# A hybrid convolution and pooling trunk on one core: turning the second group's frames on VectorE by way of memory, with two weight pieces finished by accumulating transfers

## Chip, cores and metric

One core of a Trainium2 chip runs the whole program. The metric is the device time of one execution, in microseconds; the time before is the median of three runs. A profiled execution has a span (first to last instruction) and a time of its own, which is a little longer.

## What is computed

One layer over 2,048 frames of a new stream and 32 frames of a running one, 1,024 channels each:

```python
hn = rmsnorm(h, g_mix)
hA, bA, cA, zA, vB, zB = split(hn @ w_in)              # six projections of 512 columns
u = cA * hA;  c = causal width-3 convolution of u       # yA = bA * c * silu(zA)
pooled = trailing mean of vB over 2, 4, 8 or 16 frames - vB
yB = (pooled @ pool_w[group]) * pool_scale * silu(zB)   # four groups of 128 channels
h = h + concat(yA, yB) @ w_out
h = h + (p @ w_ple) * sigmoid(rmsnorm(h, g_ple) @ w_ple_gate)
y = rmsnorm(h, g_final)
```

Besides y, the last rows of u and vB of both streams are returned.

## The kernel before

**Numbers.** Each float32 operand of a product is split into an upper part (the value cast to fp32r, by ScalarE) and a lower part (value minus upper part, by VectorE); `split` at L76 issues both. A product is three matmuls: upper by upper, upper by lower, lower by upper.

**Frames.** The 2,080 frames are five blocks of 416 columns, in three groups: blocks 0 and 1, blocks 2 and 3, block 4 (with the running stream). For the input projections a group's normalized frames must stand transposed in SBUF, channels on partitions. For a two-block group they are kept as seven operands with four quarters combined (halves of the channels by the two blocks): 11, 21, 22 and four differences T1 to T4, each split.

**Units and pairs.** A group has four units j, one for each 128 columns of every projection. A unit's six projections are made in three pairs, zb/v, c/h and za/b (`pair`, L859). A pair takes seven *half products* (`half_product`, L560) of 12 matmuls of 416 columns instead of eight, into three PSUM banks X, Y and Z. The weights' seven pieces (11, 12, S2, S1, S3, S4, 22) are made from two raw tiles of 512 KB by `pair_weights` (L521): differences on VectorE, then a split into a piece of a ring of seven buffers (`wr`); raw tiles come from a ring of four (`raws`). ScalarE's `carry` (L871) and VectorE's `out` (L874) read the banks between the products; TensorE goes on accumulating into a bank only after they have read it. Unit 0 of the first group (`plain`) multiplies in the ordinary way.

**The second group's frames.** While units 1 to 3 of the first group run, the generator `next_columns` (L1049) prepares the seven operands of the second group, 128 columns at a time, first the short last column (32 frames of each block), then columns 0, 1 and 2. `at_pace(..., 39, 62)` at L1154 advances it between half products. A column goes: load the frames of both blocks, sum of squares on ScalarE, root on GpSimd, scaling in place on VectorE (`normal`, L407), 16 transposes on TensorE into PSUM (`turn` and `four`; 8 for the short column), then the differences and seven splits, each written to memory by GpSimd (`to_memory`, L482). At the start of the second group, `load_group` loads the operands back. Frames, turned tiles and staged splits share a ring of five 4 KB slots (`xin`).

**The third group's frames** go another way already (`last_block`): `scaled_to_memory` (L1091) scales in four strided parts and writes to memory, `from_memory` (L1102) reads the rows back so that each 32-row block lies in the partitions where it belongs, and `turned_in_place` (L1110) turns all 32x32 blocks with one VectorE instruction.

**Pooling weights.** `pool_w` is loaded at once, 256 KB, and split in `vectors` (L660); `mix` (L719) multiplies a unit's pooled values with it, three matmuls a block.

**Order.** The program is written in one order, and a scheduler with its own costs puts the instructions of each engine into the order in which they run; `keep_in_program_order` holds single instructions to the written order. On the chip every engine, and each DMA queue (SP's and GpSimd's), issues strictly in that order.

Of the kernel before, what the change touches and what calls it, by code (L numbers as in the profile page):

```python
# [9 lines left out]
F32 = mybir.dt.float32  # L10
# [19 lines left out]
EARLY = 3  # L30
LATE = 2
LATER = 4


@with_exitstack
def trunk(ctx, tc, x_p, x_s, c_conv, c_pool, p_p, p_s, g_mix, w_in, conv_w, conv_b, pool_w,
# [29 lines left out]

    def rstd_of(ssq, n, name, r=None):

        ms = sm.tile([P, 1], F32, tag="ms", name=f"ms_{name}")
        nc.gpsimd.tensor_scalar(ms[:n], ssq[:n], scalar1=1.0 / D, scalar2=EPS,  # L70
                                op0=ALU.mult, op1=ALU.add)
# [259 lines left out]
    with ExitStack() as s1:  # L331
# [21 lines left out]
        def ftile(name):  # L353
            return wk.tile([P, KH, P], F32, tag="f", bufs=4, name=name)
# [73 lines left out]
        def four(xs, tag):  # L428

            for half in range(2):  # L430
                if len(xs) == 2:
                    yield [turn(x, half, f"pt_{tag}_{i}_{half}", later=True) for i, x in enumerate(xs)]
                else:
                    t = turn(xs[0], half, f"pt_{tag}_{half}", later=True)
                    yield [t[:, :, :DEC], t[:, :, DEC:2 * DEC]]

        def frame_sums(xs, tag, dst):
# [20 lines left out]
            p21, p22 = next(steps)  # L458
            nc.scalar.copy(f21, p21)
            sub(f1, p22, f1)  # L460
            sub(f12, p22, f12)
            dst("21", p21, n)
            yield
            dst("22", p22, n)
            yield
            dst("T2", f1, n)
            sub(f21, f21, f1)
            yield
            dst("T3", f12, n)
            yield  # L470
            dst("T4", f21, n)
            yield


# [7 lines left out]

        def to_memory(mem, name, src, at, n, t=None, later=False):
            t = t or staged(name)[:, :, :, :n]
            ins = put(t, src)
# [44 lines left out]
        def pair_weights(gi, ka, kb, j, name, ring, s_ring):  # L530

            s_t = (wk.tile([P, KH, P], F32, tag="s", bufs=1, name=f"s_{name}") if s_ring is None else
                   s_ring(f"s_{name}"))
            ra = raw_weight(ka, j, f"{name}a", ring)
            a11, a12 = ra[:, :KH], ra[:, KH:]
            sub = lambda o, x, y: nc.vector.tensor_tensor(o, x, y, op=ALU.subtract)
            rb = raw_weight(kb, j, f"{name}b", ring)  # L540
            a21, a22 = rb[:, :KH], rb[:, KH:]
            ins = nc.vector.tensor_tensor(s_t, a21, a22, op=ALU.add)
            if (gi, ka, j) == (1, "za", 0):
                tc.keep_in_program_order(ins)
            sub(a21, a11, a21)
            s3 = a21
            src = {"11": a11, "12": a12, "S2": a11, "S1": s_t, "S3": s3, "S4": a12, "22": a22}

            def make(q):
                if q == "S2":  # L550
                    sub(a11, s_t, a11)
                if q == "S4":
                    sub(a12, a12, a11)
                t = wtile(f"w_{name}_{q}")
                put(t, src[q])
                return t

            return make
# [84 lines left out]


        vec = const.tile([P, 112], F32, name="vec")
        pw = one.tile([P, 2, 4, P], F32R, name="pw")
# [9 lines left out]
        def vectors():  # L656
            pv = tbank("pv")
            tc.keep_in_program_order(nc.tensor.transpose(pv[:, :112], rows, ident[:112, :112]))
            nc.vector.tensor_copy(vec, pv[:, :112])
            split(pw[:, 0], pw[:, 1], pw_raw)  # L660

        cw = lambda r, j: vec[:, r * 4 + j:r * 4 + j + 1]
        cb = lambda j: vec[:, 12 + j:13 + j]
# [4 lines left out]
        pw_raw = raws.tile([P, 4, P], F32, tag="t", name="raw_pw")  # L668
        nc.sync.dma_start(pw_raw, pool_w[0].rearrange("g c d -> c g d"))

        def etile(name, n=NB):
            return wk.tile([P, 2 * NB + 16], F32, tag="e", bufs=2, name=name)[:, :n]
# [1 line left out]
        class Unit:  # L674


            def __init__(self, gi, tbs, j):
                self.gi, self.tbs, self.j, self.tag = gi, tbs, j, f"{gi}_{j}"
                self.L = min(SEQ - tbs[0] * NB, len(tbs) * NB)
                self.last = tbs[-1] == 4  # L680
                self.pooled = None
                t = lambda name, n: big.tile([P, n], F32, tag=name, name=f"{name}_{self.tag}")
# [32 lines left out]
            def store(self, chunk, b, t):  # L715
                r = self.tbs[b] * NB
                nc.sync.dma_start(y_d[chunk, :, r:r + NB], self.cols(t, b))

            def mix(self, b):  # L719

                pp, j = self.cols(self.pooled.rearrange("p h n -> p (h n)"), b), self.j
                pq = self.pooled[:, 1, b * NB:b * NB + NB]
                pm = tbank(f"pm_{self.tag}_{b}")
                nc.tensor.matmul(pm[:, :NB], pw[:, 0, j], pp, start=True, stop=False)
                nc.tensor.matmul(pm[:, :NB], pw[:, 0, j], pq, start=False, stop=False)
                nc.tensor.matmul(pm[:, :NB], pw[:, 1, j], pp, start=False, stop=True)
# [132 lines left out]
            def pair(self, ka, kb, B, D, done, ring, s_ring=None):  # L859
# [34 lines left out]
                yield  # L894
                half_product(X, make("22"), B["T4"], False)
                done[1, 0](X[:, :NB])
                yield

            def seven(self, B, aside, both=False):
# [54 lines left out]
                while i < 3:  # L954
# [4 lines left out]
                    for n in range(8):  # L959
                        for st in steps:  # L960
                            next(st)
                            aside()
                        if n == (0 if both else LATER):
                            while i and late:
                                tc.keep_in_program_order(split(*late.pop()))
                        if both and i == 2 and n == 3:
                            for b in range(2):
                                self.mix(b)
# [78 lines left out]
        def next_columns(*cs):  # L1047

            load_ahead(1, cs[0])  # L1049
            for c, after in zip(cs, cs[1:] + (None,)):  # L1050

                places = iter(t[:, :, :, i * DEC:(i + 1) * DEC] for t in map(staged, ("short_0", "short_1")) for i in range(4))
                dst = lambda q, src, n: to_memory(p_d[q], f"{q}_1_{c}", src, c * P, n, next(places) if n == DEC else None, True)
                for i, _ in enumerate(frame_sums(ahead.pop((1, c)), f"g1_{c}", dst)):
                    if after is not None and i in (6, 7):
                        load_half_ahead(after)
                    yield

# [69 lines left out]
        for gi, tbs in enumerate(GROUPS):  # L1128
# [17 lines left out]
            for j in range(4):  # L1146
                unit = gi * 4 + j
                u = Unit(gi, tbs, j)
                if unit == 0:
# [452 lines left out]
```

## Time and profile before

| | us |
|---|---|
| median of 3 runs (lowest to highest) | 926.43 (925.31 to 927.96) |
| the profiled execution's own time | 927.1 |
| its span | 925.3 |
| unit 1 of the first group begins | 78.5 |
| second group begins | 232.7 |

The profile's rows name the line, the engine (PE = TensorE, PEld its weight loads, DVE = VectorE, ACT = ScalarE, POOL = GpSimd, SP = SyncE's DMA queue), the operation and the tiles. A timeline row starts with the start and the length in us; the length of several merged instructions runs from the first start to the last end. In rows of waits the numbers are the total in us, how often, and the longest. A row of a stretch gives each engine's busy us with the number of instructions, the granted TensorE clock, the DMA engines' share and GB/s.

### The profile page before, as it was taken

Reading aid. Unit: us, or ns where it says so; the run is one execution under the profiler, and the core shown is the slowest. Engines: PE = TensorE matmul, PEld = TensorE weight load, DVE = VectorE, ACT = ScalarE, POOL = GpSimd, SP = SyncE. Lnnn points to the kernel's source line nnn. Section 1 sums busy time; section 2 is a strip of 40 time slices with the busy share of each in tenths; the row PEclk is TensorE's granted clock in tenths of the full one; section 3 lists DMA queues with packets and bytes.
Section 4 is the critical chain, followed back from the end, with each engine's and each line's share of the span. In section 5 each row is a group of like instructions: output and inputs, shape, how many; then the busy total and the mean of one; then the engine's idle time right before and its main releaser. Section 6 shows DMA issues by size and latency. Waiting matters only on the chain. (4 is left out here: it accounts for less than half of the span.)

```text
span 925.3 us, 12917 instructions
## 1 busy us (share of the span) xinstructions
PE 907.0 (98%) x4479; PEld 819.9 (89%) x4479; DVE 722.8 (78%) x1225; ACT 476.2 (51%) x880; POOL 152.8 (17%) x276
## 2 busy tenths in 40 slices
PE   7999999999999999999999999999999999999996
PEld 5999999999999999999999987888877868888884
DVE  6896898999488989785777679665554799888965
ACT  6744556554345455443545456334334776565554
POOL 3110222312001111000000010111111002333324
PEclk8999999999999999999999999999999999999998
DMA  8345555859955646357755359756775886799882
GB/s 245 87 152 153 167 160 178 265 154 317 411 165 174 191 155 189 100 180 277 201 169 173 125 192 289 263 186 177 251 220 167 292 259 160 190 232 232 227 240 91
DMA packets 140654, 186.37 MB, mean 201 GB/s; under 512 B 12044, under 2 KB 111244, under 8 KB 139309
## 3 DMA queue, kind: packets, MB, share of 16 engines
q1 hardware_dynamic: 120093, 126.07, 44.4%
q0 software_dynamic: 17760, 53.97, 19.8%
q10 hardware_dynamic: 2736, 5.51, 1.8%
q8 instruction: 35, 0.57, 0.3%
q14 instruction: 30, 0.25, 0.1%
HBM read 128.93 MB, written 56.56 MB: 200 GB/s over the span
## 5 line engine op out<-in xcount | busy, mean ns | idle before, releaser
L78 ACT CAST y_S<-y_fS 128x512 fp32r<-128x512 f32 x32 | 19.5, 621 | 41.9 <-PE x_o L168 18.9
L103 PE MATMUL e<-wq,pps 128*128 128x512 f32 (+1 forms) x156 | 38.9, 399 | 0.2 <-ACT pps L78 0.2
L168 PE MATMUL x_o<-wo_b,y_S 128*128 128x512 f32 x128 | 35.8, 391 | 0.0
L168 PE MATMUL x_g<-wg_b,g_S 128*128 128x512 f32 x128 | 35.7, 389 | 0.0
L564 PE MATMUL x_zbv<-B,w_zbv_S 128*128 128x416 f32 x168 | 34.2, 352 | 0.0
L564 PE MATMUL x_zab<-B,w_zab_S 128*128 128x416 f32 x168 | 34.1, 351 | 0.0
L564 PE MATMUL x_ch<-B,w_ch_S 128*128 128x416 f32 x168 | 34.1, 351 | 0.0
L564 PE MATMUL z_zab<-B,w_zab_S 128*128 128x416 f32 x168 | 34.0, 351 | 0.0
L564 PE MATMUL z_zbv<-B,w_zbv_S 128*128 128x416 f32 x168 | 34.0, 351 | 0.0
L564 PE MATMUL z_ch<-B,w_ch_S 128*128 128x416 f32 x168 | 34.0, 350 | 0.0
L103 PEld LDWEIGHTS e<-wq,pps 128*128 128x128 f32 (+1 forms) x156 | 27.4, 182 | 6.9 <-ACT pps L78 0.5
L1391 POOL DMA_DIRECT2D e<-h_d x28 | 24.8, 907 | 52.3 <-DVE e L1388 45.3
L70 POOL TENSOR_SCALAR ms_x<-ssq_x 128x1 f32<-128x1 f32 (+2 forms) x18 | 10.7, 592 | 127.5 <-ACT junk L89 127.2
L564 PEld LDWEIGHTS z_zbv<-B,w_zbv_S 128*128 128x128 f32 x168 | 31.4, 188 | 0.3
L564 PEld LDWEIGHTS z_zab<-B,w_zab_S 128*128 128x128 f32 x168 | 31.4, 188 | 0.3
L564 PEld LDWEIGHTS z_ch<-B,w_ch_S 128*128 128x128 f32 x168 | 31.4, 188 | 0.3
L564 PEld LDWEIGHTS x_zab<-B,w_zab_S 128*128 128x128 f32 x168 | 31.3, 188 | 0.4
L564 PEld LDWEIGHTS x_ch<-B,w_ch_S 128*128 128x128 f32 x168 | 31.3, 188 | 0.3
L564 PEld LDWEIGHTS x_zbv<-B,w_zbv_S 128*128 128x128 f32 x168 | 31.3, 188 | 0.4
L78 ACT CAST y<-y 128x512 fp32r<-128x512 f32 x24 | 14.8, 619 | 29.6 <-PE x_o L168 14.0
L168 PEld LDWEIGHTS x_o<-wo_b,y_S 128*128 128x128 f32 x128 | 23.9, 188 | 5.2 <-ACT c_o L1194 0.3
L168 PEld LDWEIGHTS x_g<-wg_b,g_S 128*128 128x128 f32 x128 | 24.0, 188 | 5.0
(582 smaller groups left out, 2649.9 us busy)
## 6 DMA issues: line engine op xcount, KB each, us to landing
y<-y_d SPq DMA_DIRECT2D x16, 512.0 KB, 6.3
x<-in_x_prompt_dram SPq DMA_DIRECT2D x16, 512.0 KB, 5.5
h_d<-x SPq DMA_DIRECT2D x16, 512.0 KB, 2.6
hn<-h_d SPq DMA_DIRECT2D x61, 128.0 KB, 6.7
xt<-in_x_prompt_dram SPq DMA_DIRECT2D x15, 512.0 KB, 7.4
e<-e_d SPq DMA_DIRECT2D x15, 512.0 KB, 5.9
e<-h_d POOLq DMA_DIRECT2D x28, 256.0 KB, 6.8
out_dram<-e POOLq DMA_DIRECT2D x14, 512.0 KB, 3.9
```

What stands on the lines that cost most here:

```text
L70: nc.gpsimd.tensor_scalar(ms[:n], ssq[:n], scalar1=1.0 / D, scalar2=EPS, op0=ALU.mult, op1=ALU.add)
L78: ins = nc.scalar.copy(hi, src)
L103: nc.tensor.matmul(ps[:n], pps[:, a, k, :n], wp[k][b][:, cs], start=k + q == 0, stop=k == 1 and q == 2)
L168: nc.tensor.matmul(ps[:n], lhs[:, k, a, :n], w[b][:, k], start=start and k + q == 0, stop=k == KH - 1 and q == 2, skip_group_check=True)
L564: nc.tensor.matmul(ps[:, :NB], lhs[:, k, x], b[:, k, y], start=start and k + q == 0, stop=stop and k == KH - 1 and q == 2, skip_group_chec ...
L1391: nc.gpsimd.dma_start(ee, h_d[r:r + P, at[1] * NH:at[1] * NH + NH], accum_op=ALU.add)
```

## The change

It has four parts.

1. **Frames of the second group.** `frame_sums` no longer uses TensorE: each frame tile is scaled by `scaled_to_memory` (four strided parts, a write of the tile), read back by `from_memory` (four loads of 128 KB) and turned by one VectorE instruction. `four` is gone, and with it 56 transposes, and ScalarE's two copies out of PSUM a column; the differences are formed from SBUF, in four tiles. The memory tile `xs_d` grows from 416 to 1,664 rows. The pace of the generator goes from 39 to 43 of 62.
2. **Slots.** `xin` has six buffers instead of five, and the tag `ms` four of its own.
3. **Pooling weights.** Each of the twelve units loads its own 64 KB and splits them: in units of pairs beside the late splits of the pooled values, else in `mix`.
4. **Two weight pieces.** In the first group's pairs, pieces S3 and 22 get their lower part otherwise: ScalarE casts the upper part, then writes its negative into the lower part, and a transfer issued by GpSimd adds the raw values to it in SBUF. They are made earlier in the written order: S3 after the product of S2, 22 after that of S1.

```diff
+BY_SUM = "S3", "22"
...
-        xin = frames_in.enter_context(tc.tile_pool(name="xin", bufs=5, side="right"))
+        xin = frames_in.enter_context(tc.tile_pool(name="xin", bufs=6, side="right"))
...
+        whole = lambda t: t.rearrange("p k (g t) -> p k g t", t=32)
+        def frame_sums(xs, tag, rows, dst):
             xs = [x_stat(x, True) for x in xs]
             yield
-            for x in xs:
-                normal(x)
+            for x, r in zip(xs, rows):
+                scaled_to_memory(x, r)
                 yield
+            ts = [from_memory(r, x[1]) for x, r in zip(xs, rows)]
+            yield
             n = P if len(xs) == 2 else DEC
-            f12, f1, f21 = (ftile(f"{c}_{tag}")[:, :, :n] for c in ("f12", "f1", "f21"))
+            f1, f2, f3, f4 = (whole(ftile(f"f{c}_{tag}")[:, :, :n]) for c in range(1, 5))
             sub = lambda o, x, y: nc.vector.tensor_tensor(o, x, y, op=ALU.subtract)
-            steps = four(xs, tag)
-            p11, p12 = next(steps)
-            nc.scalar.copy(f12, p12)
-            sub(f1, f12, p11)
+            u = turned_in_place(ts[0])
+            p11, p21 = u[:, :KH, :n // DEC], u[:, KH:, :n // DEC]
             dst("11", p11, n)
             yield
+            if len(xs) == 2:
+                u = turned_in_place(ts[1])
+            else:
+                u = u[:, :, 1:]
+            p12, p22 = u[:, :KH], u[:, KH:]
+            sub(f1, p12, p11)
             dst("T1", f1, n)
...
+                if gi == 0 and q in BY_SUM:
+                    hi, lo = t[:, :, 0], t[:, :, 1]
+                    nc.scalar.copy(hi, src[q])
+                    nc.scalar.mul(lo, hi.bitcast(F32), -1.0)
+                    nc.gpsimd.dma_start(lo.bitcast(F32), src[q], accum_op=ALU.add)
+                else:
+                    put(t, src[q])
...
+                self.pw = one.tile([P, 2, P], F32R, tag="pw", name=f"pw_{self.tag}")
+                self.pw_raw = one.tile([P, P], F32, tag="pr", name=f"pr_{self.tag}")
+                nc.sync.dma_start(self.pw_raw, pool_w[0, j])
...
                 half_product(X, make("S2"), B["T2"], False)
                 carry(X, (0, 1))
+                w = {"S3": make("S3")} if self.gi == 0 else {}
                 yield
                 half_product(Z, make("S1"), B["T1"], True)
                 carry(Z, (1, 1))
+                if self.gi == 0:
+                    w["22"] = make("22")
                 yield
-                half_product(X, make("S3"), B["T3"], False)
+                half_product(X, w.get("S3") or make("S3"), B["T3"], False)
...
-        xs_d = tc.dram_tile([NB, D], F32, name="xs_d")
+        xs_d = tc.dram_tile([4 * NB, D], F32, name="xs_d")
...
-                    aside = at_pace(next_columns(3, 0, 1, 2), 39, 62)
+                    aside = at_pace(next_columns(3, 0, 1, 2), 43, 62)
```

More of the change, by code (lines that the diff above doesn't have):

```diff
@@ L67, in rstd_of @@
     def rstd_of(ssq, n, name, r=None):
-        ms = sm.tile([P, 1], F32, tag="ms", name=f"ms_{name}")
+        ms = sm.tile([P, 1], F32, tag="ms", bufs=4, name=f"ms_{name}")
         nc.gpsimd.tensor_scalar(ms[:n], ssq[:n], scalar1=1.0 / D, scalar2=EPS,
@@ L426, in columns_in @@
             return [x_load(f"{a}_3", [x_rows(a, 3), x_rows(b, 3)])]
[L428 to L437, printed above, removed]
+        whole = lambda t: t.rearrange("p k (g t) -> p k g t", t=32)
+        def frame_sums(xs, tag, rows, dst):
             xs = [x_stat(x, True) for x in xs]
             yield
-            for x in xs:
-                normal(x)
+            for x, r in zip(xs, rows):
+                scaled_to_memory(x, r)
                 yield
+            ts = [from_memory(r, x[1]) for x, r in zip(xs, rows)]
+            yield
             n = P if len(xs) == 2 else DEC
-            f12, f1, f21 = (ftile(f"{c}_{tag}")[:, :, :n] for c in ("f12", "f1", "f21"))
+            f1, f2, f3, f4 = (whole(ftile(f"f{c}_{tag}")[:, :, :n]) for c in range(1, 5))
             sub = lambda o, x, y: nc.vector.tensor_tensor(o, x, y, op=ALU.subtract)
-            steps = four(xs, tag)
-            p11, p12 = next(steps)
-            nc.scalar.copy(f12, p12)
-            sub(f1, f12, p11)
+            u = turned_in_place(ts[0])
+            p11, p21 = u[:, :KH, :n // DEC], u[:, KH:, :n // DEC]
             dst("11", p11, n)
             yield
+            if len(xs) == 2:
[4 more added lines that the diff above has]
+            sub(f1, p12, p11)
             dst("T1", f1, n)
             yield
[L458 to L461, printed above, removed]
+            sub(f2, p22, f1)
+            sub(f3, p22, p12)
             dst("21", p21, n)
             yield
+            sub(f4, p21, f2)
             dst("22", p22, n)
             yield
-            dst("T2", f1, n)
-            sub(f21, f21, f1)
+            dst("T2", f2, n)
             yield
-            dst("T3", f12, n)
+            dst("T3", f3, n)
             yield
-            dst("T4", f21, n)
+            dst("T4", f4, n)
             yield
@@ L484, in to_memory @@
             t = t or staged(name)[:, :, :, :n]
-            ins = put(t, src)
+            v = whole if len(src.shape) == 4 else lambda a: a
+            ins = split(v(t[:, :, 0]), v(t[:, :, 1]), src)
             if later:
@@ L645, in trunk @@
         vec = const.tile([P, 112], F32, name="vec")
-        pw = one.tile([P, 2, 4, P], F32R, name="pw")
         rows = ftile("rows").rearrange("p k n -> p (k n)")[:112, :P]
@@ L659, in vectors @@
             nc.vector.tensor_copy(vec, pv[:, :112])
-            split(pw[:, 0], pw[:, 1], pw_raw)
         cw = lambda r, j: vec[:, r * 4 + j:r * 4 + j + 1]
@@ L681, in __init__ @@
                 self.pooled = None
+                self.pw = one.tile([P, 2, P], F32R, tag="pw", name=f"pw_{self.tag}")
+                self.pw_raw = one.tile([P, P], F32, tag="pr", name=f"pr_{self.tag}")
+                nc.sync.dma_start(self.pw_raw, pool_w[0, j])
+                self.pw_whole = True
                 t = lambda name, n: big.tile([P, n], F32, tag=name, name=f"{name}_{self.tag}")
@@ L717, in store, with pool_weights @@
                 nc.sync.dma_start(y_d[chunk, :, r:r + NB], self.cols(t, b))
+            def pool_weights(self):
+                if self.pw_whole:
+                    self.pw_whole = False
+                    split(self.pw[:, 0], self.pw[:, 1], self.pw_raw)
             def mix(self, b):
+                self.pool_weights()
+                pw = self.pw
                 pp, j = self.cols(self.pooled.rearrange("p h n -> p (h n)"), b), self.j
@@ L723, in mix @@
                 pm = tbank(f"pm_{self.tag}_{b}")
-                nc.tensor.matmul(pm[:, :NB], pw[:, 0, j], pp, start=True, stop=False)
-                nc.tensor.matmul(pm[:, :NB], pw[:, 0, j], pq, start=False, stop=False)
-                nc.tensor.matmul(pm[:, :NB], pw[:, 1, j], pp, start=False, stop=True)
+                nc.tensor.matmul(pm[:, :NB], pw[:, 0], pp, start=True, stop=False)
+                nc.tensor.matmul(pm[:, :NB], pw[:, 0], pq, start=False, stop=False)
+                nc.tensor.matmul(pm[:, :NB], pw[:, 1], pp, start=False, stop=True)
                 z = self.cols(self.zs, b)
@@ L894, in pair @@
                 yield
-                half_product(X, make("22"), B["T4"], False)
+                half_product(X, w.get("22") or make("22"), B["T4"], False)
                 done[1, 0](X[:, :NB])
@@ L965, in seven @@
                                 tc.keep_in_program_order(split(*late.pop()))
+                                self.pool_weights()
                         if both and i == 2 and n == 3:
@@ L1053, in next_columns @@
                 dst = lambda q, src, n: to_memory(p_d[q], f"{q}_1_{c}", src, c * P, n, next(places) if n == DEC else None, True)
-                for i, _ in enumerate(frame_sums(ahead.pop((1, c)), f"g1_{c}", dst)):
-                    if after is not None and i in (6, 7):
+                rows = (NB + c * P, 2 * NB + c * P) if c < 3 else (3 * NB,)
+                for i, _ in enumerate(frame_sums(ahead.pop((1, c)), f"g1_{c}", rows, dst), 3 - len(rows)):
+                    if after is not None and i in (8, 9):
                         load_half_ahead(after)
```

3 lines of the change are left out of this document (removed).

## The prediction

> **What bounds the kernel now.** I read the page's totals and slices, then what TensorE waited for, then engine sums by stretch, then timelines of TensorE and VectorE where the second group's frames are turned.
>
> ```profile
> PE 907.0 (98%) x4479; PEld 819.9 (89%) x4479; DVE 722.8 (78%) x1225; ACT 476.2 (51%) x880; POOL 152.8 (17%) x276
> DVE  6896898999488989785777679665554799888965
> ```
> ```profile
> PE pt L416 <- DVE xt L407: 3.2, 2, 2.3
> PE gm L376 <- DVE V L704: 2.3, 1, 2.3
> PE pt L416 <- issue: 1.3, 1, 1.3
> PE x_ch L564 <- DVE U L874: 0.9, 1, 0.9
> ```
> TensorE is busy 98% of the span, and once the opening is over its longest wait is 0.9 us: whatever leaves its queue shortens the run, and whatever makes it wait lengthens it. That one wait is on VectorE, so the sums of the stretch from units 1 to 3 of the first group come next: first unit 1 up to the pooling products of its conv pair, then **stretch R** (from there to the split of the piece S2 of unit 3's za/b pair), then the rest of the group.
>
> ```profile
> core 0: us, PE busy (x) PEld busy (x) DVE busy (x) ACT busy (x) POOL busy (x), PEclk, DMA share, GB/s
> 78.47:112.32 33.85, 33.85 (x183) 32.84 (x182) 26.59 (x51) 16.76 (x36) 6.72 (x9) 1.00 0.58 171
> 112.32:218.33 106.01, 105.14 (x575) 102.84 (x574) 99.48 (x166) 62.13 (x114) 26.73 (x33) 1.00 0.67 199
> 218.33:232.66 14.33, 14.33 (x77) 14.19 (x76) 14.26 (x24) 6.05 (x11) 3.23 (x6) 1.00 1.01 362
> 232.66:273.00 40.34, 40.34 (x215) 39.84 (x215) 24.60 (x43) 15.93 (x29) 0.54 (x1) 1.00 0.78 294
> ```
> In R VectorE is busy 99.48 of 106.01 us: two engines are full there, TensorE and VectorE, and VectorE has 6.53 us in hand. The granted clock is 1.00 throughout, so no term below is a clock term.
>
> **What leaves TensorE.** 56 transposes go: six lots of 8 and, for the short column, two of 4.
>
> ```profile
> 87.63 0.46 PE L416 MATMUL pt_g<-ident,xt 64*128 64x64 f32 x4
> 88.02 2.53 PE L564 MATMUL x_zbv<-B,w_zbv_S 128*128 128x416 f32 x12
> 90.39 2.43 PE L564 MATMUL z_zbv<-B,w_zbv_S 128*128 128x416 f32 x12
> ...
> 155.07 1.04 PE L416 MATMUL pt_g<-ident,xt 128*128 128x128 f32 x8
> 155.86 2.51 PE L564 MATMUL x_ch<-B,w_ch_S 128*128 128x416 f32 x12
> 158.21 2.43 PE L564 MATMUL z_ch<-B,w_ch_S 128*128 128x416 f32 x12
> ```
> A half product (12 matmuls) starts 2.27 us after the one before (221.33 to 223.60, quoted below). Eight transposes take 0.79 us of starts, and the product behind them 2.35 instead of 2.27: 0.87. Four short ones: 0.39 and 0.10, 0.49. Together 6 x 0.87 + 2 x 0.49 = **6.2 us**, the most the change can win on TensorE beside the 0.9 us wait above. 0.98 of it lies ahead of R.
>
> **What VectorE gains and loses inside R.** The order of the changed program's instructions says what lies inside R; the durations are start-to-start steps of these rows.
>
> ```profile
> 178.76 1.28 DVE L407 SCALAR_TENSOR_TENSOR xt<-xt,rstd_x,g_bc 128x1024 f32<-128x1024 f32 x1
> 179.96 0.58 DVE L874 TENSOR_TENSOR V<-z_zab,V 128x416 f32<-128x416 f32 x1
> ...
> 209.32 0.68 DVE L79 TENSOR_TENSOR w_ch<-raw_ch_3b,w_ch 128x512 fp32r<-128x512 f32 x1
> 209.92 0.68 DVE L79 TENSOR_TENSOR w_zab<-raw_zab_3a,w_zab 128x512 fp32r<-128x512 f32 x1
> ...
> 217.66 0.67 DVE L79 TENSOR_TENSOR w_zab_S<-raw_zab_3a,w_zab_S 128x512 fp32r<-128x512 f32 x1
> 218.26 1.07 DVE L773 SCALAR_TENSOR_TENSOR c_s<-U,vec,c_s 128x832 f32<-128x832 f32 x1
> 219.25 0.67 DVE L79 TENSOR_TENSOR w_zab_S<-s_zab,w_zab_S 128x512 fp32r<-128x512 f32 x1
> ```
> ```profile
> 301.56 1.66 DVE L1098 SCALAR_TENSOR_TENSOR xs<-xt,rstd_x,g_bc 128x256 f32<-128x256 f32 x4
> 303.64 1.23 DVE L1112 STREAM_TRANSPOSE xb<-xb 128x1024 f32<-128x1024 f32 x1
> 304.80 1.25 DVE L79 TENSOR_TENSOR w_zab<-raw_zab_1a,w_zab 128x512 fp32r<-128x512 f32 x2
> ```
> - Gone: 11 of the 18 subtractions for pieces S3 and 22 (the other 7 lie outside R), each 0.60 (209.32 to 209.92): -6.6.
> - New: 6 turns of 128x1024 at 1.16 (303.64 to 304.80): +7.0.
> - Scaling in four strided parts, about 1.60 (busy 1.66 less one overlap) instead of 1.20 (178.76 to 179.96), six times: +2.4.
> - Two splits of a unit's own pooling weights, estimated at 0.2 each from the short splits' quarter size: +0.4.
> - Moved into R by the new order: the two convolution steps of unit 3 at 1.0, one eviction at 0.5 and one split at 0.6: +3.1.
>
> Differences and splits of the frames keep their count (four and seven a column), though the sources are now SBUF. Sum: **+6.3 us**. VectorE's R is then 99.5 + 6.3 = 105.8 us of work. Over the whole group the change is nearly even for VectorE (-10.8 +7.6 +2.8 +0.8): the savings lie partly in unit 1, where it is not short of time (26.59 busy of 33.85), and the added work lies in R, where it is.
>
> Who reads it: in R's last pair TensorE cannot go on without the lower half of S2. It now starts that product 3.0 us after VectorE has finished the split:
>
> ```profile
> 221.33 2.43 PE L564 MATMUL x_zab<-B,w_zab_S 128*128 128x416 f32 x12
> 223.60 2.43 PE L564 MATMUL z_zab<-B,w_zab_S 128*128 128x416 f32 x12
> ...
> 232.66 2.43 PE L564 MATMUL x_zbv<-B,w_zbv 128*128 128x416 f32 x12
> ```
> R begins at 112.3 - 1.0 = 111.3. With the same idle time, 6.5, VectorE finishes S2 at 111.3 + 105.8 + 6.5 = 223.6. In the new order TensorE has by then done two matmuls each of S2 and S1 and the six pooling products, so 56 matmuls are left, 56 x 0.189 = 10.6, and the group ends at 234.2 instead of 232.66: **+1.5 us**. TensorE alone would be there at 215.0 (221.33 less 6.2 and the 0.9 us wait, plus four matmuls), so the 6.2 us are won and then spent waiting for VectorE.
>
> **The accumulating transfers.** Each of 18 pieces now goes: ScalarE copies the upper half, writes its negative, GpSimd issues, the transfer adds. The nearest row is the accumulating load at the end of the kernel, as big, from memory.
>
> ```profile
> DMA to landing us min/median/max: 3.7/6.8/8.6
> ```
> ```profile
> L78 ACT CAST y_S<-y_fS 128x512 fp32r<-128x512 f32 x32 | 19.5, 621 | 41.9 <-PE x_o L168 18.9
> ...
> L1391 POOL DMA_DIRECT2D e<-h_d x28 | 24.8, 907 | 52.3 <-DVE e L1388 45.3 <-DMA hn<-h_d 4.0 <-issue 3.1
> ```
> A piece's buffer (one of seven, seven pieces a pair) comes free when the same piece of the pair before has been used, six products of 2.27 or 13.6 us ahead of its own use. Two ScalarE steps at about 0.6 (0.62 in the cast row), and 6.8 to land leave 5.6 us, so most pieces are in time. Not where GpSimd's queue puts the issue behind sums of squares: at S3 of unit 2's c/h pair it stands behind both `ms` of the next column.
>
> ```profile
> 149.22 0.19 ACT L89 ACTIVATION_READ_ACCUMULATOR junk<-xt 128x1 f32 x1
> ```
> ```profile
> 149.90 0.19 POOL L70 TENSOR_SCALAR ms_x<-ssq_x 128x1 f32<-128x1 f32 x1
> ```
> The second sum ends at 149.4; `ms` takes 0.2, so the issue starts at 149.7, or 147.0 after the 2.7 us won by then; TensorE wants the piece at 155.86 - 3.6 = 152.3. Landing in 3.7, 6.8 or 8.6 us makes it 1.6 early, 1.5 late or 3.3 late. Piece 22 of unit 3's first pair stands the same way. I take **+0.8**, half of one such wait, since VectorE catches up in it. Behind the issue on GpSimd stand both `rstd`, for them VectorE's scaling, and behind that the eviction that lets TensorE reuse its bank. The raw weights also stay until the transfer has read them, so SP's load for the pair after next comes 7 to 9 us later and the block loads queue behind it; VectorE's 6.5 us of idle time held waits for such loads before, too.
>
> The Trainium skill, "DMA: Bandwidth & Descriptors", section "Anatomy of one DMA", puts a GpSimd transfer at 2.0 us plus bytes over 436 GB/s, an estimated 2.6 us here; by that this term would be 0 and the sum 0.8 lower. The trace disagrees: its accumulating row never lands under 3.7. The skill's "VectorE: DVE Perf Modes", rules for kernel authors, says to transpose 128x128 on TensorE if PSUM will do, which speaks against the change; the trace agrees for this stage only because VectorE is the fuller engine.
>
> **What I cost at nothing.** Memory: 6 frames out and back and some 12 pieces add about 10 MB to R, under 90 GB/s on 199, and 362 were moved at full share; without that cover, a load late by a microsecond is a microsecond of VectorE. Pooling weights in groups two and three: 0.2 us a unit of VectorE, which idles 15.7 of 40.34 us after R. ScalarE: 62 of 106 us busy, loses eight copies and gains 18 negations; cover gone, its casts delay VectorE. Sixth slot, `ms` buffers: no instruction.
>
> **Sum.** +1.5 + 0.8 = +2.3 on the profiled execution's 927.1 us (span 925.3 and 1.8 around it): 929.4. The median of the runs, 926.43, is 0.7 below that execution, so the forecast is **928.7**.
>
> **Rivals.**
> 1. *TensorE sets the pace after all, faster.* If VectorE's 6.5 us of idle time is only slack that it gives up when pressed, S2 is ready at 217.1 with none, the group ends at 227.7, 5.0 us sooner: 921.4. The point is 2.2 us of idle: at or under that (S2 at 219.3, group end 229.9), the run is 2.8 us faster or more. For: idle steps of 0.3 to 1.0 us are waits on casts and sums. Against: the new order adds waits of the same kind (turns on block loads, scaling on `rstd`).
> 2. *Late transfers.* At 8.6 us, both badly placed pieces are 3.3 us late and the loads behind them hold VectorE as well, estimated 1.5 us: 1.5 + 6.6 + 1.5 = +9.6 at most, half of it hidden in VectorE's lag: +6, 932.4. For: pieces move in 512-byte runs where the row has 2 KB. Against: no memory is read.
> 3. *A wash.* Half the idle time goes, 3.3, and no piece is late: 1.5 - 3.3 = -1.8, 924.6.
>
> **How the numbers follow.** Forecast 0.50, rival 1 0.17, rival 2 0.16, rival 3 0.17. About 0.3% (2.8 us) is what a measurement can tell from no change: under 923.6 faster, over 929.2 slower. The forecast's own spread (926 to 931) puts 0.28 in same and 0.22 in slower; rival 1 gives 0.17 to faster, rival 2 0.16 to slower, rival 3 0.05 to faster and 0.12 to same. Faster 0.22, same 0.40, slower 0.38. The range runs from inside rival 1 to past rival 2: 922 to 934.
>
> **What would show it.** Right: no `pt_g`; VectorE busy over 94% from the first pooling products on; TensorE waiting on VectorE at unit 3's last pair, by 5 us or more; a wait on a transfer at unit 2's c/h pair; unit 1 ahead by 1 us. Wrong: TensorE without waits there (rival 1), or waits on transfers of over 3 us (rival 2).

## The result, and the profile after

The changed kernel took **969.88 us** (median of four runs, 969.44 to 971.33) against 927.11 (925.31 to 927.96) of the kernel before, run beside it: a ratio of 1.0466 [1.045, 1.0481], 43 us slower. The forecast was 928.7, the range 922 to 934. The profiled execution took 970.06 us, its span is 968.3.

First the same three views of the changed kernel: the totals with VectorE's slices; what TensorE waited for between 60 and 330 us; and the sums by stretch (length; busy time of TensorE, its weight loads, VectorE, ScalarE, GpSimd, each with instructions; granted clock, DMA share, GB/s), the first two with the bounds of the prediction's, the last two up to the start of the second group, which was at 232.66 and is at 271.13.

```profile
PE 913.5 (94%) x4423; PEld 820.2 (85%) x4423; DVE 724.4 (75%) x1246; ACT 484.7 (50%) x901; POOL 179.2 (19%) x301
...
DVE  6995888876257898978676687856645599898965
```
```profile
PE x_zab L569 <- ACT V L884: 23.8, 2, 23.2
PE x_zab L569 <- DVE w_zab_S L80: 3.8, 1, 3.8
PE x_ch L569 <- DMA w_ch_S<-raw_ch_2b: 2.4, 1, 2.4
PE z_zbv L569 <- DVE w_zbv_S L80: 2.2, 1, 2.2
PE x_zbv L569 <- DMA w_zbv<-raw_zbv_3b: 1.9, 1, 1.9
```
```profile
78.47:112.32 33.85, 33.85 (x182) 33.52 (x181) 25.81 (x53) 19.68 (x39) 12.75 (x14) 1.00 0.94 212
112.32:218.33 106.01, 97.92 (x496) 94.84 (x495) 90.52 (x159) 57.46 (x108) 37.12 (x43) 0.97 1.01 254
218.33:232.66 14.33, 8.70 (x41) 7.22 (x41) 14.33 (x23) 9.04 (x17) 8.60 (x10) 0.86 0.84 170
232.66:271.13 38.47, 14.56 (x56) 13.48 (x55) 10.75 (x20) 4.63 (x9) 2.34 (x5) 0.65 0.83 293
```

Three things are new. TensorE is idle for 54.8 us (968.3 less 913.5) where it was 18.3: 36.5 more. It is busy 6.5 us longer with 56 matmuls fewer, and the granted clock is below 1.00 wherever it waited. And the DMA engines, 0.67 busy in stretch R before, are full there (1.01) while they move only 254 GB/s, where 362 had gone with the same share.

One wait, 23.2 us, makes over half of those 36.5. Here is how it comes about: TensorE, ScalarE, SP's queue and GpSimd's, from 228 to 262 us of the changed kernel (start, length, instruction; in brackets the idle time ahead of it and what ended it).

```profile
235.61 2.04 PE L569 MATMUL z_zab<-B,w_zab_S 128*128 128x416 f32 x10
260.81 4.53 PE L569 MATMUL x_zab<-B,w_zab_S 128*128 128x416 f32 x12 [23.15 <-ACT V L884]
265.13 2.88 PE L569 MATMUL z_zab<-B,w_zab_S 128*128 128x416 f32 x12
```
```profile
259.29 0.62 ACT L79 CAST w_ch<-raw_ch_0a 128x512 fp32r<-128x512 f32 x1 [30.68 <-DMA raw_ch_0a<-in_w_in_dram]
259.82 0.54 ACT L947 ACTIVATE V<-V 128x416 f32<-128x416 f32 x1
260.27 0.48 ACT L884 COPY V<-x_zab 128x416 f32<-128x416 f32 x1
```
```profile
226.90 0.37 SPq L513 DMA_DIRECT2D raw_zab_0a<-in_w_in_dram  x1
229.39 0.37 SPq L513 DMA_DIRECT2D raw_ch_0a<-in_w_in_dram  x1
231.87 20.88 SPq L513 DMA_DIRECT2D raw_ch_0b<-in_w_in_dram  x1
```
```profile
228.09 0.84 POOL L487 DMA_DIRECT2D p_dT4b<-T  x1
228.85 0.64 POOL L501 DMA_DIRECT2D B<-p_d  x1
```

TensorE waits for the carry of V, a copy of 0.48 us. The carry stands third in ScalarE's queue, behind a cast of `raw_ch_0a`, a weight tile of the *next* group's second pair. That tile was asked for at 229.39, half a microsecond after GpSimd began to ask for the second group's operands (1,664 KB each), and its cast waits until 259.29. The kernel before asked for it at 210.68, ahead of the operand loads:

```profile
210.68 0.43 SPq L514 DMA_DIRECT2D raw_ch_0a<-in_w_in_dram  x1
211.51 2.74 SPq L514 DMA_DIRECT2D raw_ch_0b<-in_w_in_dram  x1
```
Why it is asked for later, SP's own waits between 210 and 235 us in the changed kernel show:

```profile
SPq L513 <- DMA w_zab<-raw_zab_3b: 12.1, 1, 12.1
...
SPq L513 <- DMA p_dT<-T: 2.1, 1, 2.1
```
The load ahead of it in the queue, `raw_zab_0a`, waited 12.1 us (until 226.90) for an accumulating transfer that still read a raw tile; then `raw_ch_0a` itself waited 2.1 us more, until a piece of the second group's last column was written to memory and its slot was free.

In the kernel before only the za/b tiles, asked for at 222.85 and 223.45, met the operand loads. The landing of the first of them there:

```profile
DMA to landing us min/median/max: 33.0/33.0/33.0
```
It took as long and cost TensorE nothing: ScalarE stood 4.4 us for it, at 255.9, and nothing that TensorE needed soon stood behind that cast.

### The profile page after: what moved, and what is told of

It is laid out like the page before. It is cut to its first block, busy times and chain, and to the rows that moved or that the text cites. A ratio compares the mean times of both kernels' runs of the same rounds, so it can differ in the third digit from the quotient of the medians.

```text
span 968.3 us, 12974 instructions
## 1 busy us (share of the span) xinstructions
PE 913.5 (94%) x4423; PEld 820.2 (85%) x4423; DVE 724.4 (75%) x1246; ACT 484.7 (50%) x901; POOL 179.2 (19%) x301
## 5 line engine op out<-in xcount | busy, mean ns | idle before, releaser
L569 PE MATMUL x_zab<-B,w_zab_S 128*128 128x416 f32 x168 | 38.1, 378 | 27.6 <-ACT V L884 23.8
L569 PEld LDWEIGHTS x_zab<-B,w_zab_S 128*128 128x128 f32 x168 | 34.0, 206 | 29.6 <-ACT V L884 24.7
L921 DVE TENSOR_TENSOR c_s<-c_s,V 128x416 f32<-128x416 f32 x14 | 8.2, 586 | 28.6 <-ACT V L947 28.3
```

The costliest lines, as they stand in the source:

```text
L569: nc.tensor.matmul(ps[:, :NB], lhs[:, k, x], b[:, k, y], start=start and k + q == 0, stop=stop and k == KH - 1 and q == 2, skip_group_chec ...
L921: mul = lambda o, x, y: nc.vector.tensor_tensor(o, x, y, op=ALU.mult)
```

## Theories

- **A.** The pair's load is late, and a late load holds an in-order queue in which TensorE's work stands. It is late because the pair's raw tiles take slots of the frames' ring, which the second group's last column now releases late.
- **B.** The accumulating transfers do it: as traffic that fills the DMA engines (B2), or by holding raw tiles, so that the next raw loads are issued late (B1).
- **C.** VectorE is overloaded, as the prediction had it, only more.
- **D.** The small pooling-weight loads hold up SP's queue.

## Experiments

Each was timed beside the kernel before (whose medians were 925.6 to 927.0, so a difference of 1 us between rows means little); the last two columns are of its profiled execution.

| kernel | us | ratio [95% interval] | TensorE idle | busy |
|---|---|---|---|---|
| before | 927.1 | 1 | 18.3 | 907.0 |
| changed | 969.9 | 1.0466 [1.045, 1.0481] | 54.8 | 913.5 |
| e1 frames by memory alone | 948.1 | 1.023 [1.0186, 1.0275] | 34.7 | 908.6 |
| e2 transfers alone | 949.2 | 1.0253 [1.019, 1.0316] | 31.4 | 911.7 |
| e3 pooling weights alone | 929.1 | 1.0029 [1.0014, 1.0044] | 17.4 | 908.8 |
| e4 changed, pair first | 950.2 | 1.0272 [1.0217, 1.0326] | 36.3 | 910.9 |
| e5 = e2, fifth raw slot | 933.3 | 1.0081 [1.0055, 1.0107] | 21.3 | 910.0 |
| e6 = e2, plain copies | 940.2 | 1.0151 [1.0123, 1.0178] | 25.9 | 912.7 |
| e7 pieces by GpSimd | 934.6 | 1.0091 [1.0068, 1.0115] | 22.7 | 910.2 |
| e8 = e1, pair first | 941.6 | 1.0162 [1.0144, 1.018] | 32.0 | 908.9 |
| e9 pieces ahead, nothing else | 932.0 | 1.0058 [1.0043, 1.0073] | 20.0 | 910.5 |
| e10 changed, fifth raw slot | 968.3 | 1.046 [1.0439, 1.0481] | 54.1 | 912.3 |
| e11 changed, both | 949.7 | 1.0253 [1.0236, 1.027] | 36.9 | 910.2 |
| e12 changed, faster pace | 951.9 | 1.0288 [1.0269, 1.0307] | 37.8 | 912.0 |
| e13 = e8, no frame sums | 944.3 | 1.0207 [1.0184, 1.023] | 30.9 | 911.5 |
| e14 = e8, no wait for store | 943.0 | 1.0178 [1.0153, 1.0204] | 31.6 | 907.1 |
| e15 = e8, loads back by GpSimd | 947.4 | 1.0226 [1.0195, 1.0257] | 34.7 | 911.7 |
| e16 = e13 and e14 | 940.6 | 1.0149 [1.0127, 1.0171] | 29.5 | 910.6 |

### The parts by themselves, and the late pair

**e1**, the changed kernel without the transfers:

```diff
-BY_SUM = "S3", "22"
+BY_SUM = ()
-                w = {"S3": make("S3")} if self.gi == 0 else {}
+                w = {}
-                if self.gi == 0:
-                    w["22"] = make("22")
```


> The changed kernel with the pieces S3 and 22 split by VectorE at their own places again; the frames by memory, the sixth slot and the pooling weights by unit stay. Theory B (the 12 accumulating transfers between 112 and 228 us fill the 16 DMA engines: 57.1% against 35.8% of them on GpSimd's queue, 2 us of all 16 for each, so every load of that stretch is late): the DMA share there falls from about 1.0 to about 0.8, raw_ch_0a is issued before 217 us, ScalarE's wait of 30.7 us for it is gone, and what is left is the 11 subtractions at 0.68 that go back to VectorE: 930 to 938 us. Theory A (the frames' own trip through memory makes the second group's last column late, whatever else moves): the 30 us wait stays, 960 to 975 us. Theory C (VectorE is overloaded and that makes the column late): 7.5 us more on VectorE, 975 us or more.

**e2**, the kernel before with that part of the change alone (the block with `accum_op`, the two pieces made ahead; four slots for `ms`, as in e5, e6, e7 and e9):

> The kernel before with one edit: S3 and 22 of units 1 to 3 finished by accumulating transfers; TensorE still turns the second group's frames. Theory B: the DMA share of 112 to 218 us rises from 0.67 to about 0.9; if that is enough to make the column's writes and the raw loads late, 940 us or more. Theory A: the column is made by TensorE and needs no load back, raw_ch_0a is issued before 214 us, VectorE has 6.6 us less to do: 921 to 929 us.

**e3**, the kernel before with `pool_weights`, the sixth slot and four slots for `ms`. (Without the last it does not fit in SBUF: 1.91 KB a partition are wanted where 1.78 are left.)

> The kernel before with the pooling weights loaded by unit, the sixth slot for frames and four slots for ms, nothing else. Theory A, B and C: nothing to see, 925 to 929 us. Theory D (the small loads, which wait on SP's queue up to 8.1 us in the changed kernel, hold up the loads behind them): 935 us or more.

**e4**, the changed kernel with the pair's two raw tiles loaded ahead of the operands:

```diff
+        def load_first_pair():
+            for kind, end in (("c", "a"), ("h", "b")):
+                t = spare_ring(f"raw_ch_1_0{end}")
...
+                ins = nc.gpsimd.dma_start(t, w_in[:, col:col + P].rearrange("(k p) n -> p k n", p=P))
             if gi == 1:
-                B = load_group(1)
+                u = Unit(gi, tbs, 0)
+                with tc.issue_after(load_first_pair().ins):
+                    B = load_group(1)
```


> The changed kernel with the raw weights of unit (1,0)'s c/h pair loaded on GpSimd's queue, ahead of the second group's operand loads. Theory A as to the stall (the load is late only because it meets the 11.6 MB of operand loads): raw_ch_0a lands within 8 us of its issue, ScalarE's wait of 30.7 us falls under 8, the operands come some 6 us later, and of the 43 us lost 20 to 30 come back: 940 to 950 us. If instead the DMA engines are the bound there in any order, the operands are late by what the pair is earlier, TensorE waits for them, and 960 us or more is left.

Measured: 948.1, 949.2, 929.1 and 950.2 us. e3 is 2.9 us slower (0.29%): D explains nothing of this size. e4 fits A as to the stall: ScalarE's wait falls from 30.7 to 11.3 us (under 8 was expected), TensorE's from 23.2 to 7.0, and 20 us come back, though the tile still takes 13.4 us to land (8 were expected). e1 fits no theory, and e2 only B's time (940 or more): the DMA share of 112 to 218 us, 0.9 by B, is 0.77 there. Each half alone costs 21 to 22 us. That the two add up to the whole is chance: with the pair loaded first, the frames alone cost 15 us (e8, below) and the whole 23 (e4), so the transfers add 8 there, not 22, and the late pair the other 20.

e2 shows one way. This is VectorE's wait for a raw tile, SP's issue of it, and ScalarE's and TensorE's waits behind it, in e2:

```profile
151.84 0.69 DVE L543 TENSOR_TENSOR s_zab<-raw_zab_2b 128x512 f32<-128x512 f32 x1 [7.65 <-DMA raw_zab_2b<-in_w_in_dram]
...
153.18 0.58 DVE L881 TENSOR_TENSOR zs<-z_zbv,zs 128x416 f32<-128x416 f32 x1
```
```profile
136.75 1.39 SPq L515 DMA_DIRECT2D raw_zab_2b<-in_w_in_dram  x1
```
```profile
153.80 0.55 ACT L921 ACTIVATE zs<-zs 128x416 f32<-128x416 f32 x1 [7.92 <-DVE zs L881]
...
157.77 0.49 ACT L878 COPY c_s<-x_ch 128x416 f32<-128x416 f32 x1
```
```profile
158.31 3.83 PE L571 MATMUL x_ch<-B,w_ch_S 128*128 128x416 f32 x12 [6.96 <-ACT c_s L878]
```
A tile that landed 15 us after its issue stops VectorE at a sum for a pair that comes later; the eviction of `zs` stands behind it; ScalarE's activation waits for the eviction, and the carry that TensorE needs stands behind the activation. It is A's mechanism at another place: three engines in line behind one load, none of them needing it for the product at hand.

### What of the transfers costs

**e5** gives raw weights the slot that the frames had got (`raws` 4 to 5, `xin` stays 5, pooling weights by unit):

> The pieces alone (949 us), with a fifth slot for raw weights in the place of the sixth for frames, paid for by the pooling weights by unit. Theory B1 (a raw tile stays held until the transfer has read it, so the raw load that takes its slot is issued late: raw_zbv_3a at 153 us, and VectorE stands 7.6 us before s_zab at 152): with a slot more the loads are issued earlier by a tile's life, both waits of 4.6 and 7.0 us go, 925 to 933 us. Theory B2 (the transfers fill the DMA engines themselves; raw_zab_2b was issued at 137 and landed at 152): a slot more doesn't make a transfer shorter, 940 us or more.

**e6** replaces the accumulating transfer by a plain copy (`accum_op=ALU.add` taken out, so the sum is left out):

> The pieces alone (949 us), with plain copies in the place of the accumulating transfers: same bytes, same issues, same holders. It leaves out the sum, so the low halves of S3 and 22 are wrong. Theory B2 in its narrow form (the adding at the far end is what takes the engines' time): the DMA share of 130 to 148 us falls from 1.05 to below 0.8, 925 to 933 us. Theory B1, or B2 with the 512 B packets as the price: the same 943 to 952 us.

**e7** lets GpSimd subtract (`split(hi, lo, src[q], nc.gpsimd)`):

> The kernel before with the same pieces S3 and 22 of units 1 to 3 finished by a subtraction on GpSimd, made one product ahead as the transfers are. No transfer, no raw tile held by one. If the gain of relieving VectorE is there to be had at all, and GpSimd's subtraction takes under 2.3 us (a product's time): 921 to 926 us. If GpSimd takes longer or holds VectorE up: 930 us or more. Theory A and B give no number of their own here.

**e9** makes the two pieces ahead and lets VectorE subtract (`split(hi, lo, src[q])`):

> The kernel before with the pieces S3 and 22 of units 1 to 3 made a product ahead, as the change makes them, and finished by VectorE as before: neither transfer nor GpSimd. If what the transfers leave over with a fifth raw slot (7 us) and what GpSimd's subtractions cost (8 us) is the price of making pieces ahead (tiles of the ring of 7 held longer, other orders on ScalarE and VectorE): 931 to 936 us. If making them ahead is free: 925 to 928 us.

Measured: 933.3 (the upper end of B1's forecast), 940.2 (between both), 934.6, 932.0. GpSimd's queue between 112 and 215 us, ahead of the operand loads (packets, MB, share of 16 engines), in the kernel before, in e2 and in e6, and below e2's and e6's the landing of all their transfers:

```profile
q0 software_dynamic: 2736, 9.96, 32.6%
```
```profile
q0 software_dynamic: 7138, 10.34, 46.8%
```
```profile
DMA to landing us min/median/max: 4.2/5.4/8.7
```
```profile
q0 software_dynamic: 3217, 11.47, 37.4%
```
```profile
DMA to landing us min/median/max: 2.7/3.5/7.3
```
A megabyte on the queue takes 3.3 of these points before and in e6, and 4.5 in e2. If the rest of e2's bytes go in packets as before (275 a megabyte), its ten accumulating transfers of that time make some 5,000 packets, about 500 for each 256 KB, so 512 B each. A plain copy of the same piece makes few packets and lands in 2.7 to 7.3 us instead of 4.2 to 8.7; that is worth 8 of e2's 22 us (each kernel against the one before that ran beside it). The fifth slot is worth 15, so holding the raw tile is the larger part, and the two overlap. What is left of e5 (7.2 us) is no more than what e3 and e9 cost by themselves (2.9 and 5.6), and e9 has no transfer: making the pieces ahead has a price of its own. e9's ScalarE and TensorE:

```profile
137.92 0.62 ACT L79 CAST T<-f_g 128x512 fp32r<-128x512 f32 x1 [3.63 <-DMA p_d<-21_1_0_1375]
138.44 0.50 ACT L876 COPY zs<-x_zbv 128x416 f32<-128x416 f32 x1
```
```profile
134.50 2.43 PE L569 MATMUL z_zbv<-B,w_zbv_S 128*128 128x416 f32 x12
138.99 3.56 PE L569 MATMUL x_zbv<-B,w_zbv_S 128*128 128x416 f32 x12 [2.07 <-ACT zs L876]
142.35 2.98 PE L569 MATMUL z_zbv<-B,w_zbv_S 128*128 128x416 f32 x12
```
In the new order a carry stands behind a cast into a frame slot that a write to memory still holds. e7's subtractions take 1.3 to 1.8 us each on GpSimd and add 2.6 us to e9. So taking 0.6 us pieces off VectorE won nothing in any form tried.

### What of the frames by memory costs

**e8** is e1 with e4's pair first, **e10** the changed kernel with e5's slots (`xin` 6 to 5, `raws` 4 to 5), **e11** both:

> The frames by memory without the transfers (948 us), with unit (1,0)'s c/h raw weights loaded on GpSimd's queue ahead of the second group's operands. In the frames by memory alone VectorE stood 5.9 us for raw_ch_0b, TensorE 5.3 us behind it, and some 2 us more went to the lower clock after it. Theory A': that wait is one part of the loss there, the rest (7.1 and 3.3 us of waits for VectorE's splits, and their clock) is VectorE's own load: 939 to 943 us. If the operands come later by what the pair comes earlier: 946 to 950 us.

> The changed kernel with the slot moved from the frames (six to five) to the raw weights (four to five). Theory B1 (raw tiles held by the transfers make the loads late): the 16 us that this gave back to the pieces alone come back here as well or more, since the load of the pair is then earlier too: 945 to 957 us. If the frames by memory need the sixth slot, or the stall comes from the frames alone: 962 us or more.

> The changed kernel with both: the fifth raw slot in the place of the sixth for frames, and the c/h raw weights ahead of the second group's operands on GpSimd's queue. If the two losses are separate ones, 16 and 20 us come back: 932 to 938 us. If both cure the same late load: 945 to 952 us.

Measured: 941.6, as expected; 968.3 and 949.7, hardly other than without the fifth raw slot (969.9, 950.2). In the whole change that slot does not help: the pair's tiles come from the frames' ring, and in e10, where that ring has lost the slot, VectorE still waits 25.0 us for `raw_ch_0b`. What decides there is the last column. **e12** asks for it earlier:

```diff
-                    aside = at_pace(next_columns(3, 0, 1, 2), 43, 62)
+                    aside = at_pace(next_columns(3, 0, 1, 2), 43, 54)
```


> The changed kernel with the columns of the second group put out at 43 steps in 54 calls instead of 62, so that the last column is asked for 8 products, some 18 us, earlier. Theory A'' (the pair's load is late because the last column's pieces, whose slots it takes, are written at 223 to 228 us): raw_ch_0a is issued before 220 us, ahead of the operand loads, and the stall of 23 us goes or falls under 6: 940 to 952 us. If VectorE and the DMA engines cannot bring the column sooner, or the loads before it are pushed back instead: 960 us or more.

Measured 951.9, at the upper end of what A foresaw; `raw_ch_0a` was asked for at 223.04 instead of 229.39 (before 220 was foreseen), and the 23 us stall is gone, for a wait of 7.6 us elsewhere. So A holds for the stall: the pair waits for the column's slots, and 6 us in that issue decide 18 us of the run.

Left are the 15 us that e8 costs without transfers and without the late pair (e3's 2.9 among them). TensorE's longest waits in e8 are mostly for VectorE's splits:

```profile
PE y_zbv L578 <- DVE w_zbv L80: 6.7, 1, 6.7
PE y_zab L578 <- DVE w_zab L80: 3.3, 1, 3.3
PE x_ch L578 <- ACT c_s L893: 2.9, 1, 2.9
```
which looked like C. **e13** writes the second group's pieces without their sums (`dst("T1", p12, n)` and so on, the `sub` calls taken out); **e14** loads the tiles to be turned from the input instead of `xs_d`; **e15** issues those loads on GpSimd's queue; **e16** is e13 with e14:

> The frames by memory without the transfers and with the pair's weights first (942 us), with the second group's four sums of each column left out (their pieces written from unsummed quarters, so the second group's outputs are wrong): 16 subtractions of about 0.65 us less on VectorE. If what is left of that kernel's loss is VectorE's own load (waits of 6.7 and 3.3 us for its splits): 7 to 12 us come back, 928 to 936 us. If it is the trip through memory or the clock: 938 us or more.

> The frames by memory without the transfers and with the pair's weights first (942 us), the tiles to be turned loaded from the input instead of the scaled copy: the scaling, its store and all other work stay, only the load no longer waits for the store (so the second group's frames are unscaled, and its outputs wrong). Theory L (the trip's latency, with SP's queue standing for the store, pushes the weight loads and splits behind it back): 928 to 936 us. Theory V (the instructions that the trip adds to VectorE and the transfers themselves): 939 to 944 us.

> The same kernel (942 us) with the second group's loads back issued on GpSimd's queue instead of SP's, so that no raw weight load stands behind them on SP's. Theory L: 930 to 938 us. Theory V: 939 to 944 us; above that, if eight issues of about 0.9 us for each column hold up the writes behind them on GpSimd's queue.

> The frames by memory without the transfers and with the pair's weights first (942 us), with both taken away at once: the second group's frame sums (16 subtractions on VectorE) and the load's wait for the store of the scaled frames; the second group's outputs are wrong. Each alone gave nothing back (944 and 943 us). If VectorE's load and the trip's latency are two limits of one height, one behind the other: 925 to 935 us. If neither is what costs these 15 us, but the added transfers or the order in which the engines' instructions stand: 939 to 945 us.

Measured: 944.3, 943.0, 947.4, 940.6. C fell, and so did the latency of the trip (L), alone and together. With VectorE 7.3 us less busy (733.0 to 725.7) the waits of 6.7 and 3.3 us went and others came in their place. In e16 ScalarE's longest is

```profile
ACT T L79 <- DMA p_dT<-T: 12.1, 4, 3.6
```
casts into frame slots that writes still hold. With the rows for the other pieces such waits are 14.2 us in e16, 6.7 in e8, and none in the kernel before. That points to the ring of frame slots, in which the changed kernel keeps four more tiles of a column (two scaled, two to be turned) for one slot more. Shown is only that VectorE's sums and the wait for the store, alone or together, do not account for the 15 us, nor does the place of the loads in SP's queue. Three rivals were not tried: a ring of more slots (the memory is full), the trip's own transfers (half of e14's theory V, into whose range 943.0 falls; the DMA share in R is 0.76 in e8, against 0.67), and the order of the instructions, which the scheduler makes anew for every variant. The cause of these 15 us stays open.

## Why the prediction was wrong, by its own steps

- **Transposes** (6.2 us won): right as far as it can be seen. 4,423 matmuls instead of 4,479, no `pt_g`, and unit 1 is ahead (its last c/h product starts at 106.83 instead of 109.11: 2.3 us, where 1 was said).
- **VectorE in R** (105.8 us of work and "the same idle time, 6.5"): the work was right, the idle time was not, so VectorE was not the bound. From the last pooling product of unit 1 to the end of S2's split VectorE was busy 106.5 us and idle 15.6:

```profile
110.03:232.07 122.04, 108.37 (x546) 103.81 (x545) 106.48 (x186) 67.81 (x125) 45.42 (x52) 0.96 0.99 241
```
  It waited 5.1 us for ScalarE's casts of frame pieces (2.1 before), 2.3 for a product, 1.9 for `rstd`, 1.6 for a raw tile. So S2 was ready at 232.1 where 223.6 was said, and TensorE waited 3.8 us for it where at least 5 were said. In the stretch with the old bounds VectorE was 85% busy, under the 94% that would have shown it full.
- **Accumulating transfers**: the places were right (2.4 us at unit 2's c/h pair, 1.9 at unit 3's first; 1.5 to 3.3 late was said). The price was not. The text saw that raw tiles stay until the transfer has read them and that "block loads queue behind it", and let VectorE's 6.5 us of idle time cover that. **This is the step that failed**, with the two terms of the next point: late loads were priced at nearly nothing. That time covers a late load once, while each load behind it is late too, and so is all that stands behind its first reader. Alone, the transfers cost 22 us (e2), and one slot for raw weights gave 15 of them back (e5); in the changed kernel 22 us come back without them (e1).
- **What was costed at nothing.** *Memory* was judged by bytes (under 90 GB/s on 199, 362 moved at full share). The engines were full at 254 GB/s: share, not bytes, is what ran out, and the accumulating transfers spend more of it per byte (e2 against e6). *Sixth slot* had no instruction and so no price; but its ring also holds the next group's c/h weights, and that late pair, worth some 20 us (e4, e12), is the largest single term of the 43.
- **The order ahead** (not costed at all): making two pieces earlier costs 5.6 us (e9, with the four slots for `ms`).
- **"No term below is a clock term"**: wrong once there are waits. Of the 12.7 us that matmuls are longer (6.5 busy, 6.2 not done), about 9 lie ahead of the second group (TensorE busy 227.7 to 271.13, against 224.9 to 232.66 before). The other 3.7 lie late in the run, where the same matmuls go 1.5% slower (262 against 266 in 60 us, both at a granted clock of 1.00); this was not followed up.
- **Rivals**: rival 2, late transfers, named the right kind of event and priced it at +6. It counted 3.3 us twice for the products at hand and only 1.5 us for all the loads behind them, where much of the loss lay.

The Trainium skill's figure that the prediction weighed ("DMA: Bandwidth & Descriptors", section "Anatomy of one DMA"; an estimated 2.6 us for 256 KB from GpSimd) is close to e6's fastest plain copy, 2.7; the accumulating one never landed under 4.2.

## What to carry to other kernels

Where every engine's queue is in order, ask of each load that an edit makes later not who needs it but what stands behind its first reader: a 0.5 us carry behind a cast of the *next* stage's tile cost 23 us here. Judge spare DMA capacity by the share of engine time, not by GB/s, and follow a ring of buffers to everything that draws from it, the next stage's loads too. An edit that holds a buffer longer to save 0.6 us of a full engine needs another buffer before it can pay (here it did not pay even then: e5 is 7 us slower than the kernel before).

## What was not expected of the hardware

TensorE's waits cost more than their length. In e1 it stands for 7 us, and then (timeline of TensorE; below it, sums of 6 us each, the granted clock third from the end):

```profile
185.63 3.83 PE L569 MATMUL y_zbv<-B,w_zbv 128*128 128x416 f32 x10 [7.05 <-DVE w_zbv L80]
189.26 3.13 PE L569 MATMUL x_zbv<-B,w_zbv_S 128*128 128x416 f32 x12
192.22 2.43 PE L569 MATMUL z_zbv<-B,w_zbv_S 128*128 128x416 f32 x12
```
```profile
172.00:178.00 6.00, 6.00 (x33) 5.95 (x32) 6.00 (x12) 2.29 (x4) 1.99 (x3) 1.00 0.96 303
...
184.00:190.00 6.00, 4.37 (x13) 4.18 (x14) 5.54 (x12) 4.87 (x9) 3.62 (x6) 0.50 1.00 286
190.00:196.00 6.00, 6.00 (x31) 5.91 (x30) 6.00 (x13) 1.68 (x4) 1.14 (x2) 0.94 0.56 203
```
The 22 matmuls behind the wait take 6.6 us (185.63 to 192.22) where 22 at 0.189 take 4.2: 2.4 us for a wait of 7. In e9 a wait booked at 2.07 cost 12 matmuls 1.1 us (3.56 for 2.43) and the next 12 another 0.55. The Trainium skill has the rule, "TensorE: Matmul & The Clock Gate", section "Part 1: The HAM clock gate": after an idle window of about 3.4 us the clock falls to half until the array has been busy for about as long. The 0.50 above agrees with it. e9 does not quite: its clock is still 1.00 when the products start again, and then

```profile
140.50:143.50 3.00, 3.00 (x10) 2.86 (x10) 2.28 (x5) 1.56 (x4) 0.00 (x0) 0.50 1.09 363
```
behind an idle time of 2.07 us, shorter than the rule's; here the measurement decides.

A load of 512 KB on SP's queue took 33.0 us (kernel before) and 29.9 (changed kernel, from 229.39 to the cast that waited for it) beside operand loads of 1,664 KB on GpSimd's, where such loads took 3.7 to 5.2 us earlier in the first group; and an accumulating transfer of 256 KB holds GpSimd 1.3 us at issue, where a plain copy of it takes 0.8 (e6).
